# Weight products of 256 columns read from other places in SBUF, and eight transpose groups moved behind the last gate's rows

## The chip, the cores and the metric

One core of a Trainium2 chip runs the whole program in one launch. The metric is device time in microseconds (us). The kernel before takes 2344.75 us as the median of three runs (2341.22, 2344.75 and 2345.06).

## The reference

A two-layer trunk on x of 256 tokens by 2048 features, all in float32. Each layer is a mixer and an MLP, each of them ahead of it normed, scaled and shifted by a conditioning vector:

```
for l in (0, 1):
    sh1, sc1, g1, sh2, sc2, g2 = split(silu(c) @ ada_w[l] + ada_b[l], 6)
    h = rms_norm(x, norm1_g[l]) * (1 + sc1) + sh1
    x = x + g1 * mixer_l(h)          # layer 0: mLSTM and retention heads; layer 1: sparse attention
    h = rms_norm(x, norm2_g[l]) * (1 + sc2) + sh2
    x = x + g2 * (square(relu(h @ mlp_w1[l])) @ mlp_w2[l])     # 2048 -> 8192 -> 2048
```

Most of the work is products of h with weight matrices of 2048 rows, the widest of them mlp_w1 and mlp_w2.

## The kernel before, in words

**Two-part products.** Activations lie transposed: a tile `hs` holds for 128 features the 256 tokens twice, columns 0 to 255 the high part (float32 rounded to fp32r) and columns 256 to 511 the low part (the rest). A weight tile comes by DMA into `raw` (128 rows, up to 1024 columns), ScalarE rounds it into `wh` (L232) and VectorE writes the rest into `wl` (L234), both in `wsplit`. A product then takes high by high, high by low and low by high. There are two forms of it, and all their matmuls have line L124:

- `tmul`: 128 weight columns from `wh` are loaded into TensorE and multiply the 512 columns of `hs`; then 128 from `wl` multiply its first 256. Two matmuls, "a pair" below. The first MLP product and most of the second of layer 0 run so.
- `nmul2`: three matmuls of 256 columns, `wh` by the high part, `wh` by the low part, `wl` by the high part. "A triple" below. The mixers' projections into and out of the heads (`segment`, `out_groups`, the index and query products of layer 1), the first products of a layer's part (`entry`) and two of eight tiles of `residual` in layer 0's MLP run so.

In `nmul` (the value columns in `linear_n` and at L1116 on, and all of `result`) the weights are the moving operand instead, 512 columns at a time.

**Places.** The `hs` tiles, the `wh` tiles and the `wl` tiles all start at addresses that leave the same rest by 256 bytes. `wh` has 64 columns (256 bytes) of room beyond its 1024, and `place[0]` (L226) says how many columns behind its start the high part is written: 0 in both mixers, in layer 0's value products and in `result`, and 48 (192 bytes) in the MLPs from `entry` to the end of mlp_w1, and in layer 0 through mlp_w2. `wl` has no such room.

**Order.** Each engine runs its instructions in the order in which the program lists them. `linear` walks over pairs of 128-row blocks of the weights; after each output tile of a block it calls `side()`, which takes one entry from the list `pending` (None: do nothing). Small work is put there in pieces. `Fill` fetches the conditioning weights `ada_w` in between, one block of 512 KB per due slot, and VectorE sums them with the condition (`acc`, L402).

**The last gate.** In layer 1's MLP the last 2048 numbers of the conditioning (`ada_rows`, two halves `hf`) must stand in rows over all tokens. Each half takes two matmuls of `ones` by `acc`, in plain float32 with 512 columns (L124, shown as M<-acc,c), put into `pending` three entries apart.

**Turning the residual.** The last product leaves its output by tokens, so x, which lies by features, is turned: `turn(c)` for c from 0 to 3, each two groups of four 128 by 128 transposes (L579, M<-c,xT) with copies by ScalarE and VectorE. They are queued before mlp_w1's second column group, each behind twelve empty entries.

Of the kernel before, what the change touches and what calls it, by code (L numbers as in the profile page):

```python
# [18 lines left out]
P = 128  # L19
# [75 lines left out]
def tile_trunk(ctx: ExitStack, tc: tile.TileContext, io, out):  # L95
# [127 lines left out]
    def held_back():  # L223
        return tc.issue_after(behind[0]) if behind else nullcontext()

    place = [0]  # L226

    def wsplit(raw, n):
        wh = wp.tile([P, 1024 + 64], F32R, tag="wh", name="wh")[:, place[0]:place[0] + 1024]
        wl = wp.tile([P, 1024], F32R, tag="wl", name="wl")  # L230
        with tc.high_priority(offset=60):
            S.copy(wh[:, :n], raw[:, :n])  # L232
            with held_back():
                last_split[0] = V.tensor_tensor(wl[:, :n], raw[:, :n], wh[:, :n].bitcast(F32), op=OP.subtract)  # L234
        return wh, wl
# [9 lines left out]
            o += b - a  # L245
        return raw

    def wload(W, k0, kper, cols):

        raw = wp.tile([P, 1024], F32, tag="raw", bufs=4, name="raw")  # L250
        wfetch(raw, W, k0, kper, cols)
        return wsplit(raw, kper * sum(b - a for a, b in cols))

    def tmul(o, h, wh, wl, c, m, start, stop):

# [43 lines left out]
    def linear_n(W, nk, kper, c0_, hget, evac, fill=None, k1=0):  # L299

        bs = [lbank() for _ in range(2)]
        for k0 in range(k1, nk, kper):
            wh, wl = wload(W, k0, kper, [(c0_, c0_ + 512)])
            if fill is not None:
                fill()
            for t in range(2):
                for kk in range(kper):
                    k = k0 + kk
                    nmul(bs[t], hget(k), t, wh[:, kk * 512:(kk + 1) * 512], wl[:, kk * 512:(kk + 1) * 512],
                         k == k1, k == nk - 1)  # L310
                side()
        for t in range(2):
            evac(t, bs[t])
# [46 lines left out]
    def ada_rows(acc, hf):  # L360

        r = wp.tile([P, 1024], F32, tag="ada", bufs=3, name="grow")
        SP.dma_start(r[0:1, :], io["ada_b"][1:2, 5 * D + hf * 1024:5 * D + (hf + 1) * 1024])
        V.tensor_tensor(acc[0:1, :], acc[0:1, :], r[0:1, :], op=OP.add)

        def part(q):
            b = bank(3)
            mm(b, ones, acc[:, q * 512:(q + 1) * 512])
            S.copy(acc[:, q * 512:(q + 1) * 512], b)

        def end():
            part(1)
            grow[hf] = acc
            open_.pop(0)

        open_.append(acc)
        pending.extend([None] * 2 + [lambda: part(0), None, None, None, end])

    landing = []

# [115 lines left out]
    def entry(W, cols, tiles, norm, l, n, held, late, out, done):  # L496


        w = sum(b - a for a, b in cols)
        us = norm.plain(l, n)  # L500
        ws = []
        for k0 in range(0, 8, 2):
            tag, room = (("wh", 1088), ("wl", 1024))[k0 // 2 % 2]
            r = wp.tile([P, room], F32, tag=tag, bufs=4, name="wu")
            ws.append(wfetch(r, W, k0, 2, cols))
        norm.lengths(last_split[0].ins)
        hs, sums_ = [None] * KT, []
        for k0 in range(0, KT, 2):
            if k0 >= 8:
                wh, wl = wload(W, k0, 2, cols)  # L510
            for q, (c, m) in enumerate(tiles):
                for kk in range(2):
                    k = k0 + kk
                    if k < 8:
                        mm(held[q][0:m, 0:T + 1], ws[k0 // 2][:, kk * w + c:kk * w + c + m], us[k][:, 0:T + 1],
                           k == 0, k == 7)
                    else:
                        nmul2(q % 2)(late[q // 2], hs[k], wh, wl, kk * w + c, m, k == 8 and q % 2 == 0, k == KT - 1)
            side()
            if k0 == 6:  # L520
                for k in range(8, KT):
                    hs[k] = norm.normed(l, n, k)
                for q, (c, m) in enumerate(tiles):
                    b, s = held[q], small.tile([P, 1], F32, tag="shs", name="shs")
                    V.tensor_tensor(out[q], b[0:m, 0:T], norm.rb[0:m], op=OP.mult)
                    S.copy(s[0:m], b[0:m, T:T + 1])
                    sums_.append(s)
        behind.clear()
        for q, (c, m) in enumerate(tiles):
            V.scalar_tensor_tensor(out[q], late[q // 2][0:m, q % 2 * T:q % 2 * T + T], sums_[q][0:m], out[q],  # L530
                                   op0=OP.add, op1=OP.add)
            done(q)
        for k in range(8):
            hs[k] = norm.normed(l, n, k)
        return hs
# [56 lines left out]
    def result(W, hget):  # L592
# [2 lines left out]
        held = [lbank() for _ in range(4)] + [bank(i) for i in range(4)]  # L595
        last = []
        for k in range(n):
            w = [wload(W, k, 1, [(c, c + 1024)]) for c in (0, 1024)]
            h = hget(k)
            if k >= n - 2:  # L600
                last.append((k, h, w))
                continue
            for t in range(2):
                for c in range(4):
                    wh, wl = (v[:, c % 2 * 512:c % 2 * 512 + 512] for v in w[c // 2])
                    nmul(held[4 * t + c], h, t, wh, wl, k == 0, False)
# [11 lines left out]
    def mlp(l, before, fill, norm):  # L618
        with ExitStack() as es:
# [13 lines left out]
            def squared(i, a):  # L633
# [1 line left out]
                S.activation(z[i], a, AF.Square)  # L635

            free[:] = [3]
            place[0] = 48
            hs = entry(io["mlp_w1"][l], [(0, 512)], [(j * P, P) for j in range(4)], before, l, 1,
                       [bank(0), bank(1), bank(2), lbank()], [lbank(), lbank()], [ztile(i) for i in range(4)],  # L640
                       lambda q: squared(q, z[q]))
            if l == 1:
                for c in range(4):
                    pending.extend([None] * 12 + turn(c))
            for g in range(1, DFF // 512):
                def evac(j, b, g=g):
                    a = tmp.tile([P, T], F32, tag="half", name="half")
# [5 lines left out]
            if l == 1:  # L653
                fill.flush()
                while pending:
                    side()
                place[0] = 0
                zp.tile([P, 24], F32, name="pad")
                result(io["mlp_w2"][l],
                       lambda k: split_to_hs(z[k], zp.tile([P, 2 * T], F32R, tag="zh", bufs=3, name="zh")))  # L660
                return
            residual(io["mlp_w2"][l], DFF // P, lambda k: split_to_hs(z[k]), shift(l, 5), norm, mlp_groups(),
                     2, fill)
            place[0] = 0
            fill.flush()
            free[:] = [0, 1, 2, 3]

# [23 lines left out]
    with ExitStack() as es:  # L691
# [3 lines left out]
        def wraw(name="raw"):  # L695
            tag = turns.pop(0)
            turns.append(tag)
            return wp.tile([P, 1088 if tag == "wh" else 1024], F32, tag=tag, bufs=4, name=name)[:, 0:1024]

        xn = [[wraw("xn") for _ in range(2)] for _ in range(2)]  # L700
        for t in range(2):
# [155 lines left out]
        def gates():  # L857
# [3 lines left out]
            V.tensor_scalar(gb, gb, 1.0 / 15.0, None, op0=OP.mult)  # L861
            wg = tmp.tile([P, KT, 8], F32, tag="diag", bufs=2, name="wg")
            SP.dma_start(wg, wE[:, 4096:4104].rearrange("(k p) c -> p k c", p=P))
            wgh, wgl = wsplit(wg.rearrange("p k c -> p (k c)"), KT * 8)
            gbk = bank()
            for k in range(KT):
                tmul(gbk, hs[k], wgh, wgl, k * 8, 8, k == 0, k == KT - 1)
# [48 lines left out]
                emat.append(E)  # L916


        qk = sums(7)
        for k in range(KT):  # L920
            if k >= 12:
# [192 lines left out]
    nb = [nb[2 * i:2 * i + 2] for i in range(3)]  # L1114
    q0b = bank(2)
    for k in range(PART, KT):  # L1116
        w = [wload(wE, k, 1, wcols[:1]), wload(wE, k, 1, wcols[1:])]
        fill()
        for s in range(3):
            for t in range(2):  # L1120
# [60 lines left out]
    with ExitStack() as es:  # L1181
# [5 lines left out]
        SP.dma_start(rb_, io["rel_bias"])  # L1187
        b = bank()
        mm(b[0:16, 0:384], rb_, c3[0:32, 256:640])
        bv = ap.tile([16, 384], F32, name="bv")  # L1190
        V.tensor_copy(bv, b[0:16, 0:384])
        bd = dram.tile([16, 384], F32, name="bd")
        SP.dma_start(bd, bv)
# [201 lines left out]
```

## Time and profile before

| | |
|---|---|
| median of three runs | 2344.75 us |
| the profiled execution | 2340.88 us |
| its span on the core | 2339.1 us |
| TensorE matmul busy | 2280.5 us (97%) |
| TensorE weight loads busy | 2033.0 us (87%) |
| VectorE busy | 1704.9 us (73%) |
| ScalarE busy | 1191.6 us (51%) |
| DMA, mean | 262 GB/s |
| mean granted TensorE clock | 0.992 of full speed |

Matmuls overlap in the records: one starts before the one ahead of it has ended, and its recorded time reaches over the next. What a matmul costs in a stream is therefore the time from its start to the next start, which a count of matmuls in a stretch, or the starts in a timeline, give. A count of a stretch also holds about two matmuls that started ahead of it.

The stretches of the run: mixer of layer 0 up to 595 us (its output product from about 502), MLP of layer 0 to 1316 (mlp_w1 to 953), mixer of layer 1 to 1617 (output product from 1542), MLP of layer 1 to the end (entry to 1644, mlp_w1 to 1986, then `result`).

### The profile page before, as it was taken

The numbers are of one execution on the slowest core, as the hardware profiler recorded it, in microseconds if no ns is written. First come the engines' busy times: TensorE is split into PE (matmuls) and PEld (weight loads), VectorE is DVE, ScalarE is ACT, GpSimd is POOL, SyncE is SP. The second block draws the span as 40 slices with busy tenths as digits, with TensorE's granted clock in tenths as the row PEclk, the third lists the DMA queues.
The fourth block names the chain that finished last, engine by engine and source line by source line (L and its number), as shares of the span: only waits on it lengthen the run. The fifth ranks groups of instructions, "written<-read, shape, count | busy, mean of one in ns | idle before, by whom it ended". The sixth has DMA issues, their size and how long they took to land.

```text
span 2339.1 us, 37507 instructions
## 1 busy us (share of the span) xinstructions
PE 2280.5 (97%) x14121; PEld 2033.0 (87%) x14121; DVE 1704.9 (73%) x2499; ACT 1191.6 (51%) x2248; POOL 0.5 (0%) x8
## 2 busy tenths in 40 slices
PE   5899998999999999999999999999999999999999
PEld 3689888999988888999989899999988888888887
DVE  5768897995877777888988779865777455555555
ACT  3225455455555556655555445664655555444443
POOL 0000000000000000000000000000000000000000
PEclk8999999999999999999999999999999999999999
DMA  9998998996699999999899787645798665555554
GB/s 329 355 300 285 297 319 286 326 325 207 215 311 318 317 316 315 310 305 315 284 327 320 233 271 229 227 139 176 242 313 269 182 188 188 189 198 192 193 191 162
DMA packets 268909, 611.97 MB, mean 262 GB/s; under 512 B 26692, under 2 KB 95286, under 8 KB 268728
## 3 DMA queue, kind: packets, MB, share of 16 engines
q1 hardware_dynamic: 268728, 609.59, 78.2%
q8 instruction: 110, 1.80, 0.3%
q14 instruction: 71, 0.58, 0.1%
HBM read 607.38 MB, written 2.12 MB: 261 GB/s over the span
## 4 chain that ended last, share of the span: by engine, by line
PE 80%; DVE 9%; DMA 6%; issue 2%; ACT 2%; SPq 0%; DVEq 0%; ACTq 0%
PE L L124 49%; PE M L124 30%; DMA ada<-in_ada_w_dram 3%; DVE wl L234 3%; DMA raw<-in_even_w_in_dram 2%; DVE acc L402 1%; DVE acc L754 1%; PE M L332 1%; ACT wh L232 1%; DMA raw<-in_mlp_w_dram 1%; ACT junk L335 0%; DVE cv L1064 0%; DVE hs L207 0%; SPq L243 0%; PE M L737 0%
## 5 line engine op out<-in xcount | busy, mean ns | idle before, releaser
L234 DVE TENSOR_TENSOR wl<-raw,wh 128x1024 fp32r<-128x1024 f32 (+1 forms) x724 | 876.7, 1213 | 489.4 <-ACT wh L232 480.1
L232 ACT CAST wh<-raw 128x1024 fp32r<-128x1024 f32 (+1 forms) x724 | 753.7, 1042 | 830.6 <-PE M L124 442.1
L124 PE MATMUL L<-hs,wh 128*128 128x256 f32 (+1 forms) x4608 | 1131.7, 324 | 6.5 <-ACT wh L232 4.2
L124 PE MATMUL L<-hs,wl 128*128 128x256 f32 x3120 | 874.8, 281 | 2.4 <-DVE wl L234 2.4
L124 PEld LDWEIGHTS L<-hs,wh 128*128 128x128 f32 x4608 | 772.1, 190 | 70.9 <-ACT wh L232 5.9
L124 PEld LDWEIGHTS L<-hs,wl 128*128 128x128 f32 x3120 | 591.0, 190 | 4.1 <-DVE wl L234 3.2
L124 PE MATMUL M<-hs,wh 128*128 128x512 f32 (+2 forms) x1816 | 518.6, 347 | 0.0
L402 DVE SCALAR_TENSOR_TENSOR acc<-ada,cond,acc 128x1024 f32<-128x1024 f32 x300 | 383.3, 1278 | 30.5 <-DMA ada<-in_ada_w_dram 30.0
L124 PE MATMUL M<-hs,wl 128*128 128x256 f32 (+2 forms) x1444 | 403.1, 279 | 0.0
L124 PEld LDWEIGHTS M<-hs,wh 128*128 128x128 f32 (+1 forms) x1816 | 313.7, 187 | 52.1 <-issue 1.6
L124 PEld LDWEIGHTS M<-hs,wl 128*128 128x128 f32 (+2 forms) x1444 | 269.2, 186 | 1.9 <-issue 1.0
L124 PE MATMUL L<-wh,zh 128*128 128x512 f32 x512 | 168.7, 389 | 0.0
L124 PE MATMUL M<-wh,zh 128*128 128x512 f32 x512 | 168.6, 389 | 0.0
L124 PEld LDWEIGHTS L<-wh,zh 128*128 128x128 f32 x512 | 96.0, 188 | 20.2 <-issue 0.3
L124 PEld LDWEIGHTS M<-wh,zh 128*128 128x128 f32 x512 | 96.2, 188 | 20.0
L335 ACT ACTIVATE junk<-M 128x128 f32<-128x128 f32 x210 | 55.2, 278 | 88.0 <-PE M L332 87.9
L124 PE MATMUL L<-wl,zh 128*128 128x512 f32 x256 | 99.7, 389 | 0.0
L124 PE MATMUL M<-wl,zh 128*128 128x512 f32 x256 | 99.6, 389 | 0.0
L754 DVE SCALAR_TENSOR_TENSOR acc<-ar,cond,acc 128x512 f32<-128x512 f32 x120 | 90.2, 751 | 4.8 <-DMA ar<-in_ada_w_dram 1.0
L634 ACT ACTIVATE half<-half 128x256 f32<-128x256 f32 x120 | 47.8, 411 | 28.6 <-DVE half L325 28.6
L124 PE MATMUL L<-hf,raw 128*128 128x256 f32 x224 | 53.3, 392 | 4.9 <-DMA raw<-in_even_w_in_dram 4.9
L124 PEld LDWEIGHTS L<-wl,zh 128*128 128x128 f32 x256 | 48.1, 188 | 10.2 <-DVE wl L234 0.3
(273 smaller groups left out, 1575.4 us busy)
## 6 DMA issues: line engine op xcount, KB each, us to landing
raw<-in_mlp_w_dram SPq DMA_DIRECT2D x504, 512.0 KB, 4.6
ada<-in_ada_w_dram SPq DMA_DIRECT2D x320, 512.0 KB, 5.3
raw<-in_even_w_in_dram SPq DMA_DIRECT2D x136, 256.0 KB, 5.4
ar<-in_ada_w_dram SPq DMA_DIRECT2D x64, 512.0 KB, 7.8
raw<-in_odd_w_in_dram SPq DMA_DIRECT2D x48, 512.0 KB, 4.5
raw<-in_even_w_out_dram SPq DMA_DIRECT2D x32, 512.0 KB, 5.3
raw<-in_odd_w_out_dram SPq DMA_DIRECT2D x32, 512.0 KB, 4.2
raw<-in_even_w_in_dram SPq DMA_DIRECT2D x28, 512.0 KB, 6.1
```

The source lines that it names most:

```text
L124: PE.matmul(o, a, b, start=start, stop=stop, skip_group_check=True)
L232: S.copy(wh[:, :n], raw[:, :n])
L234: last_split[0] = V.tensor_tensor(wl[:, :n], raw[:, :n], wh[:, :n].bitcast(F32), op=OP.subtract)
L332: PE.transpose(b[:, i * P:(i + 1) * P], t, ident)
L335: S.activation(j, b[:, i * P:(i + 1) * P], func, accum_out=dst[:, i:i + 1])
L402: V.scalar_tensor_tensor(acc, r, cond[:, kr:kr + 1], acc, op0=OP.mult, op1=OP.add)
L634: S.activation(a, a, AF.Relu)
L754: V.scalar_tensor_tensor(acc, ar[:, kr], cc, acc, op0=OP.mult, op1=OP.add)
```

## The change

Two things. First, `wl` gets the same 64 columns of room as `wh`, and the place becomes a pair of numbers (columns behind the start for `wh` and for `wl`). EVEN (0, 0) stays for the products of 512 columns with the weights moving and for the gates' eight columns. WIDE (48, 0) is what the MLP's pairs had. PAIRED (16, 48), 64 and 192 bytes, is new: it holds for the triples of both mixers from the query and key products of layer 0 on, and for every `entry`. Second, the turns of the residual leave their place ahead of mlp_w1 and follow in `pending` the rows of the last gate: chunks 0 and 1 the first half's, chunks 2 and 3 the second's. A small tile of layer 1, `bv`, moves into a buffer that later holds logits, which makes room.

```
-    place = [0]
-    def wsplit(raw, n):
-        wh = wp.tile([P, 1024 + 64], F32R, tag="wh", name="wh")[:, place[0]:place[0] + 1024]
-        wl = wp.tile([P, 1024], F32R, tag="wl", name="wl")
+    ROOM = 1024 + 64
+    EVEN, PAIRED, WIDE = (0, 0), (16, 48), (48, 0)
+    place = [EVEN]
+    def wsplit(raw, n, at=None):
+        a, b = place[0] if at is None else at
+        wh = wp.tile([P, ROOM], F32R, tag="wh", name="wh")[:, a:a + 1024]
+        wl = wp.tile([P, ROOM], F32R, tag="wl", name="wl")[:, b:b + 1024]
...
     def linear_n(W, nk, kper, c0_, hget, evac, fill=None, k1=0):
-            wh, wl = wload(W, k0, kper, [(c0_, c0_ + 512)])
+            wh, wl = wload(W, k0, kper, [(c0_, c0_ + 512)], EVEN)
...
     def ada_rows(acc, hf):
-        pending.extend([None] * 2 + [lambda: part(0), None, None, None, end])
+        pending.extend([None] * 2 + [lambda: part(0), None, None, None, end, None, None])
+        for c in (2 * hf, 2 * hf + 1):
+            pending.extend(turn(c))
...
     def entry(W, cols, tiles, norm, l, n, held, late, out, done):
-                wh, wl = wload(W, k0, 2, cols)
+                wh, wl = wload(W, k0, 2, cols, PAIRED)
...
     def mlp(l, before, fill, norm):
-            place[0] = 48
+            place[0] = WIDE
...
-            if l == 1:
-                for c in range(4):
-                    pending.extend([None] * 12 + turn(c))
...
             residual(io["mlp_w2"][l], DFF // P, lambda k: split_to_hs(z[k]), shift(l, 5), norm, mlp_groups(),
-            place[0] = 0
+            place[0] = PAIRED
...
+        place[0] = PAIRED
         qk = sums(7)
...
-        bv = ap.tile([16, 384], F32, name="bv")
+        bv = ap.tile([P, 384], F32, tag="lg", bufs=3, name="bv")[0:16]
```

The places move no instruction. The turns do. On TensorE, near the start of mlp_w1 in layer 1 before, the first of eight transpose groups stands among the pairs (c_78 is the identity, hs, wh and wl as above):

```order
L124 MATMUL L<-hs,wh 128x512
L124 MATMUL L<-hs,wl 128x256
L579 MATMUL M_18170<-c_78,xT 128x128 x4
L124 MATMUL L<-hs,wh 128x512
L124 MATMUL L<-hs,wl 128x256
```

All eight groups stood so, far ahead of the gate's rows; these pairs now follow each other without a transpose. On TensorE now, from the second of the first half's two matmuls for the gate's rows (the one with acc) on:

```order
L124 MATMUL M_18995<-acc,c_78 128x512
L124 MATMUL M_18998<-hs,wh 128x512
L124 MATMUL M_18998<-hs,wl 128x256
...
L124 MATMUL M_18985<-hs,wh 128x512
L124 MATMUL M_18985<-hs,wl 128x256
L583 MATMUL M_19020<-c_78,xT 128x128 x4
L124 MATMUL M_18990<-hs,wh 128x512
L124 MATMUL M_18990<-hs,wl 128x256
```

Six pairs lie between that matmul and the first transposes, and eight pairs between the first and the second matmul of the rows. Four transpose groups follow each half's rows.

## Rows read from the trace of the kernel before

**Rows 1.** The page's chain that ended last: shares by engine, then by line.

```profile
PE 80%; DVE 9%; DMA 6%; issue 2%; ACT 2%; SPq 0%; DVEq 0%; ACTq 0%
PE L L124 49%; PE M L124 30%; DMA ada<-in_ada_w_dram 3%; DVE wl L234 3%; DMA raw<-in_even_w_in_dram 2%; DVE acc L402 1%; DVE acc L754 1%; PE M L332 1%; ACT wh L232 1%; DMA raw<-in_mlp_w_dram 1%; ACT junk L335 0%; DVE cv L1064 0%; DVE hs L207 0%; SPq L243 0%; PE M L737 0%
```

**Rows 2.** Busy time by stretch; first line names the columns, x counts instructions.

```profile
core 0: us, PE busy (x) PEld busy (x) DVE busy (x) ACT busy (x) POOL busy (x), PEclk, DMA share, GB/s
120.00:330.00 210.00, 203.30 (x1251) 180.06 (x1250) 167.55 (x239) 101.19 (x177) 0.10 (x1) 0.99 0.91 296
330.00:502.00 172.00, 163.34 (x1294) 160.10 (x1293) 153.92 (x281) 80.05 (x170) 0.00 (x0) 0.98 0.95 320
502.00:595.00 93.00, 93.00 (x769) 92.54 (x768) 58.10 (x86) 45.95 (x88) 0.00 (x0) 1.00 0.72 236
1316.00:1542.00 226.00, 222.83 (x1744) 211.51 (x1743) 192.25 (x509) 130.96 (x321) 0.00 (x0) 1.00 0.68 222
1542.00:1617.00 75.00, 75.00 (x626) 74.87 (x625) 38.71 (x54) 36.43 (x71) 0.00 (x0) 1.00 0.64 196
1644.00:1735.00 91.00, 91.00 (x545) 80.49 (x544) 69.73 (x79) 53.74 (x91) 0.00 (x0) 1.00 0.82 279
1735.00:1986.00 251.00, 251.00 (x1426) 218.74 (x1425) 143.14 (x150) 137.21 (x227) 0.00 (x0) 1.00 0.68 214
```

**Rows 3.** Chain of waits by line: 120 to 330, 330 to 502, 502 to 595, 1316 to 1542.

```profile
by line: DMA ada<-in_ada_w_dram 20.7%; PE L L124 12.4%; DVE wl L234 12.1%; PE M L124 11.7%; issue 10.9%; DMA raw<-in_even_w_in_dram 9.0%; DVE acc L402 7.6%; DVE cv L1064 4.7%; SPq L243 2.5%; DVE v L686 2.4%; ACT wh L232 1.2%; DVE mt L900 0.
by line: PE L L124 23.1%; DMA raw<-in_even_w_in_dram 15.6%; DMA ada<-in_ada_w_dram 11.4%; DVE wl L234 9.7%; issue 8.8%; DVE acc L402 6.2%; ACT wh L232 3.1%; PE M L124 2.5%; ACT junk L335 2.2%; PE M L1012 1.8%; DVE hs L207 1.4%; PE M L332 1.
by line: PE L L124 95.2%; PE M L124 2.8%; PE M L1012 1.1%; PE M L332 1.0%
by line: PE L L124 57.6%; PE M L124 9.8%; DVE wl L234 5.6%; issue 2.8%; DVE sc L1272 2.5%; ACT wh L232 1.8%; DVE m L1271 1.7%; ACT lg L1302 1.6%; PE M L332 1.5%; DVE lg L1290 1.3%; ACT lg L1299 1.2%; DVE acc L402 1.1%; DVE lg L1295 1.0%; DV
```

**Rows 4.** TensorE alone in four unbroken streams: triples, pairs, entry's triples, pairs.

```profile
core 0: us, PE busy (x), PEclk, DMA share, GB/s
550.00:590.00 40.00, 40.00 (x335) 1.00 0.61 189
700.00:750.00 50.00, 50.00 (x296) 1.00 0.92 315
1633.00:1643.00 10.00, 10.00 (x87) 1.00 0.62 170
1762.00:1812.00 50.00, 50.00 (x288) 1.00 0.82 270
```

**Rows 5.** Timeline of TensorE in layer 1's entry: start us, us, engine, line, operation.

```profile
1331.29 0.40 PE L124 MATMUL M<-hs,wh 128*128 128x256 f32 x2
...
1331.65 0.39 PE L124 MATMUL M<-hs,wh 128*16 128x256 f32 x2
...
1331.99 0.39 PE L124 MATMUL M<-hs,wh 128*16 128x256 f32 x2
```

**Rows 6.** Timeline of TensorE around the gate's first rows in mlp_w1 of layer 1.

```profile
1733.35 0.39 PE L124 MATMUL L<-hs,wh 128*128 128x512 f32 x1
...
1733.69 0.39 PE L124 MATMUL L<-hs,wh 128*128 128x512 f32 x1
...
1734.04 1.02 PE L124 MATMUL M<-acc,c 128*128 128x512 f32 x2
...
1735.24 0.40 PE L124 MATMUL L<-hs,wh 128*128 128x512 f32 x1
...
1735.60 0.40 PE L124 MATMUL L<-hs,wh 128*128 128x512 f32 x1
```

**Rows 7.** Timeline of TensorE around one transpose group, seventy microseconds earlier.

```profile
1664.64 0.60 PE L579 MATMUL M<-c,xT 128*128 128x128 f32 x4
...
1665.43 0.39 PE L124 MATMUL L<-hs,wh 128*128 128x512 f32 x1
...
1665.77 0.39 PE L124 MATMUL L<-hs,wh 128*128 128x512 f32 x1
```

More of the change, by code (lines that the diff above doesn't have):

```diff
@@ L246, in wfetch, with wload @@
         return raw
-    def wload(W, k0, kper, cols):
+    def wload(W, k0, kper, cols, at=None):
         raw = wp.tile([P, 1024], F32, tag="raw", bufs=4, name="raw")
         wfetch(raw, W, k0, kper, cols)
-        return wsplit(raw, kper * sum(b - a for a, b in cols))
+        return wsplit(raw, kper * sum(b - a for a, b in cols), at)
     def tmul(o, h, wh, wl, c, m, start, stop):
@@ L502, in entry @@
         for k0 in range(0, 8, 2):
-            tag, room = (("wh", 1088), ("wl", 1024))[k0 // 2 % 2]
-            r = wp.tile([P, room], F32, tag=tag, bufs=4, name="wu")
+            r = wp.tile([P, ROOM], F32, tag=("wh", "wl")[k0 // 2 % 2], bufs=4, name="wu")
             ws.append(wfetch(r, W, k0, 2, cols))
@@ L597, in result @@
         for k in range(n):
-            w = [wload(W, k, 1, [(c, c + 1024)]) for c in (0, 1024)]
+            w = [wload(W, k, 1, [(c, c + 1024)], EVEN) for c in (0, 1024)]
             h = hget(k)
@@ L663, in mlp @@
                      2, fill)
-            place[0] = 0
+            place[0] = PAIRED
             fill.flush()
@@ L697, in wraw @@
             turns.append(tag)
-            return wp.tile([P, 1088 if tag == "wh" else 1024], F32, tag=tag, bufs=4, name=name)[:, 0:1024]
+            return wp.tile([P, 1024 if tag == "raw" else ROOM], F32, tag=tag, bufs=4, name=name)[:, 0:1024]
         xn = [[wraw("xn") for _ in range(2)] for _ in range(2)]
@@ L863, in gates @@
             SP.dma_start(wg, wE[:, 4096:4104].rearrange("(k p) c -> p k c", p=P))
-            wgh, wgl = wsplit(wg.rearrange("p k c -> p (k c)"), KT * 8)
+            wgh, wgl = wsplit(wg.rearrange("p k c -> p (k c)"), KT * 8, EVEN)
             gbk = bank()
@@ L1116, in tile_trunk @@
     for k in range(PART, KT):
-        w = [wload(wE, k, 1, wcols[:1]), wload(wE, k, 1, wcols[1:])]
+        w = [wload(wE, k, 1, c, EVEN) for c in (wcols[:1], wcols[1:])]
         fill()
```

## The prediction, made before the changed kernel was run

> **What bounds the kernel now.** I read the chain that ended last first [rows 1]: 79% of the span is TensorE at L124, the line of all weight products, so what a product costs from its start to the next start is most of the time. The busy times by stretch come next [rows 2]: from 502 to 595 us, from 1542 to 1617 and in all of mlp_w1 of layer 1 (1644 to 1986) TensorE is busy without a gap, at a granted clock of 1.00, the 2.4 GHz level; from 120 to 502 the DMA share is 0.91 to 0.95 and TensorE has gaps. The chain of each stretch says how far a shorter product would move the end there [rows 3]: L124 is 98% of it from 502 to 595, 67% from 1316 to 1542, but 26% from 330 to 502 and 24% from 120 to 330, where DMAs, VectorE's low parts and issue make up most of the rest.
>
> Then the pace inside unbroken streams [rows 4]. About two of each count began ahead of the window. Mixer triples with both parts in the input's place: 333 in 40 us, 120 ns each, 360 per triple. Pairs in layer 0's mlp_w1: 294 in 50 us, 340 ns per pair. Both forms read 768 moving columns, so the same columns cost 20 ns more as a triple. The triples of the entry, whose high parts lie 192 bytes on and whose low parts lie in the input's place: 85 in 10 us, 117.6 each, 353 per triple. And the last row of the group: pairs of layer 1's mlp_w1, same code and same clock as the 340 ones, 286 in 50 us, 350 per pair.
>
> Two timelines say where these differences come from. In layer 1's entry, still with every part in the input's place for the small tiles, a triple with 128 weight columns starts 0.36 us ahead of the next, one with 16 weight columns 0.34 [rows 5]: the moving columns are the same, and it is the loading of weights beside them that costs the 20 ns. In mlp_w1 of layer 1 the pairs go at 0.34 until the first plain-float32 matmuls for the gate's rows, and at 0.36 (350 ns, by the count) from the first pairs behind them [rows 6]; the last of [rows 4] shows them still so, and 1735 to 1986 holds some 710 pairs in 251 us [rows 2], 353 each with the second half's rows among them. Behind a transpose group the pairs go at 0.34 [rows 7]. So there are two steady paces, and what ran last before the stream picks one.
>
> **The places.** They remove and add no instruction. Triples that get the new places: 140 in layer 0's query and key products (10 blocks of 14), 64 and 384 in its segments, 256 in its output product, 32 in layer 1's entry, 384 in its index and query products, 256 in its output product, and 64 in the two MLP entries: 1580. Pairs keep their place; the low-part buffers move by whole multiples of 256 bytes, and `wh`'s buffers, which are spaced that way already, show no pace of their own within the counted streams, so I cost this at nothing. Products with moving weights and the gates keep theirs.
>
> No row has parts at 64 and 192 bytes, so the price of a triple there is bounded. Fast side: 340, from the 16-column triple [rows 5] and the pairs [rows 4]. Slow side: 370, which is today's 360 plus the 10 ns that the slow pace adds to the pairs [rows 4]. Today's 360 and the entry's 353 lie between. The value that I take is 346.5, midway between 353 and 340: the entry's row is the nearest one, there one of the two parts is off the input's place and a third of the 20 ns is gone, and now both are. That is 13.5 ns per triple of the mixers and 6.5 per triple of the MLP entries.
>
> What of it moves the end, by the chain's shares [rows 3]: the two output products, all, 512 x 13.5 = 6.9 us. Layer 1's 416 others, 0.67 x 416 x 13.5 = 3.8. The 448 of the segments, 0.26 x 448 x 13.5 = 1.6; there a TensorE that is early waits for weights, with the DMAs at 320 GB/s and a share of 0.95 [rows 2]. The 140 ahead of them, 0.24 x 140 x 13.5 = 0.5. The entries, 64 x 6.5 = 0.4. Sum 13.2 us.
>
> Here a rule speaks against the change. The rows say that loading 128 columns instead of 16 costs the product beside it 20 ns per triple [rows 5]. The Trainium skill (TensorE: Matmul & The Clock Gate, Step-by-step: what each phase is for) says that TensorE has two independent read ports to SBUF, and that loading the next weights takes no read bandwidth from the running matmul. By it no place could matter, and this term would be 0 instead of 13.2; the trace does not agree, and I go by the trace, but the rule's outcome is the first rival below.
>
> **The turns.** Eight groups of four transposes, with eight copies of ScalarE more than VectorE's eight, leave the start of mlp_w1 and come back in the same stretch: the same number at the same price, beside pairs in both places. Their eight copies on ScalarE and four on VectorE are hidden by a TensorE that never waits there, with VectorE busy 143 of 251 us and ScalarE 137 [rows 2]; the `ada` buffers that they borrow delay the gate's weights by some steps, and the DMA share of 0.68 to 0.82 leaves room for that. If that cover went, the price would be a wait of TensorE for weights of a few us at most, since all eight groups take under 4 us of TensorE (0.45 each, by the 0.79 from the group's start to the second pair behind it less a 0.34 pair [rows 7]).
>
> What the move does change is the last thing that runs before each long stream of pairs. Now the transposes come six pairs behind the second rows matmul of each half. If they set the pace to 340 as they do in [rows 7], the slow pace lasts from the first rows matmul to the first transposes, 14 pairs, twice. Between 1735 and 1986 there are some 710 pairs (1426 matmuls [rows 2], less the rows' and the window's edge). The two paces differ by 349.7 - 340.1 = 9.6 ns [rows 4]: (710 - 28) x 9.6 = 6.5 us, all on the path. Its bounds: nothing, if the transposes only keep a fast pace and cannot restore one, since all groups that the trace shows behind pairs of mlp_w1 came into a fast stream; and 6.8 if they restore it at once.
>
> **The sum.** 13.2 + 6.5 = 19.7 us less than the profiled execution's 2340.9 gives 2321. That execution lies 3.9 below the median of the three runs; from the middle of both, 2342.8, it is **2323 us**, which I predict. Its own range is 2311 to 2332: at the fast end triples at 340, all of the gain of 1316 to 1542 and half of that of 120 to 502 (10.2 + 8.3 + 5.9 + 0.8 + 6.5 = 31.7), at the slow end the entry's 353 everywhere and 6.5.
>
> **Rivals.** First: the places do nothing, triples stay at 360. For it: in the stream of triples nothing but the start address of the weights changes, and 128 columns of 4 bytes sweep over 512 bytes wherever they start. Against it: the entry's 353 with only that changed. Time: 2342.8 - 6.5 = 2336. It is what the rule of the Trainium skill cited above would give (TensorE: Matmul & The Clock Gate, the same section).
>
> Second: the transposes do not restore the pace, or the entry's new triples hand the slow one to the pairs. For it: no row shows a slow stream that became fast within mlp_w1, and the early transposes that followed the entry are gone, so that a slow start would last from 1644 to 1735, 545 matmuls [rows 2] or, without 32 transposes, some 255 pairs, 2.5 us, and I take as much again for layer 0. Against it: the pace behind all transposes is the same. Time: 2342.8 - 13.2 = 2330, up to 2335.
>
> Third, the other side: the new places meet worse than the old. The low parts, which sat in the input's place, are the middle product's neighbours; if loading them 192 bytes on, or the high parts 64 on, keeps falling on the columns that the product beside it reads, a triple goes to 370. A longer product is covered by nothing in the output products and less by DMAs elsewhere: 576 x 10 + 0.9 x 416 x 10 + 0.7 x 588 x 10 = 13.6 us more, less 6.5: 2350. It decides from about 365 ns per triple on, where the turns' 6.5 are used up. Against it: 360 is an unvarying 120 per matmul, and the one place tried was better.
>
> Fourth: neither part does anything, 2343.
>
> **Chances.** Forecast 0.55, first rival 0.13, second 0.14, third 0.12, fourth 0.06. Range for 8 in 10: 2310, the fast end, to 2340, which takes in the first two rivals and leaves out most of the last two. A measurement tells some 0.2%, 4.7 us, from no change, so faster means below 2340.1: all of the forecast, 0.11 of the first and 0.13 of the second, together 0.79; within 0.2% 0.11 (the fourth, and the rims of the others), slower 0.10.
>
> **What would show it.** A stream of mixer triples in the output products with 343 to 355 in 40 us instead of 333 tells the first step right; still 333 tells the first rival, 325 the third. In mlp_w1 of layer 1 the starts of pairs should be 0.36 apart for two short stretches behind the rows and 0.34 from the first transposes to 1986's counterpart; 0.36 throughout tells the second rival. The output products should shrink by 3 to 5 us each, 1316 to 1542 by about 4, and 330 to 502 by less than 3, with more of TensorE's waits ended by DMAs and VectorE. I am wrong if the pairs' pace in layer 0's MLP changes, or if 120 to 502 gives back more than half of its triples' gain.

## The result, and the profile after

| | before | after |
|---|---|---|
| median of three runs | 2344.75 us | 2326.86 us (2325.87 to 2327.96) |
| the profiled execution | 2340.88 us | 2326.86 us |
| TensorE matmul busy | 2280.5 us | 2255.0 us |

The ratio is 0.9927 with a 95% interval of 0.9912 to 0.9943: 17.9 us less by the medians, 14.0 by the two profiled executions. The predicted 2323 is 3.9 us off, well within its range, but the experiments below show two of its assumptions on the places off, in opposite directions, so that part of the nearness is luck.

TensorE alone, in the kernel after: busy time with the count of matmuls, granted clock, DMA share and GB/s. The stretches stand against those of [rows 4]; the fifth is later in the same mlp_w1.

```profile
core 0: us, PE busy (x), PEclk, DMA share, GB/s
548.00:588.00 40.00, 40.00 (x353) 1.00 0.62 193
700.00:750.00 50.00, 50.00 (x297) 1.00 0.93 323
1625.00:1635.00 10.00, 10.00 (x86) 1.00 0.55 159
1746.00:1796.00 50.00, 50.00 (x296) 1.00 0.88 302
1880.00:1930.00 50.00, 50.00 (x297) 1.00 0.65 195
```

The mixers' triples: 351 matmuls in 40 us instead of 333, 114 ns each; from start to start a triple takes 340 ns, apart from one delay of 0.2 us in that window (before 360, without a delay), as low as the pairs. The gain is 19.7 ns per triple, the mean over layer 1's output product. Layer 0's pairs are as they were. Layer 1's pairs, 350 before, go at 340 in both stretches. The 10 us of the entry tell little: one matmul is 1.2% of them.

What happens around the gate's rows is the next view, a timeline of TensorE after: start, duration, line, operation.

```profile
1722.27 0.39 PE L124 MATMUL L<-hs,wh 128*128 128x512 f32 x1
...
1722.61 0.39 PE L124 MATMUL L<-hs,wh 128*128 128x512 f32 x1
...
1722.96 1.02 PE L124 MATMUL M<-acc,c 128*128 128x512 f32 x2
...
1724.17 0.40 PE L124 MATMUL L<-hs,wh 128*128 128x512 f32 x1
...
1724.52 0.40 PE L124 MATMUL L<-hs,wh 128*128 128x512 f32 x1
...
1729.59 0.60 PE L583 MATMUL M<-c,xT 128*128 128x128 f32 x4
...
1730.38 0.40 PE L124 MATMUL M<-hs,wh 128*128 128x512 f32 x1
...
1730.73 0.40 PE L124 MATMUL M<-hs,wh 128*128 128x512 f32 x1
...
1731.08 0.39 PE L124 MATMUL M<-hs,wh 128*128 128x512 f32 x1
```

Starts of pairs are 0.34 apart ahead of the first matmul for the rows and 0.35 behind it (0.36 in [rows 6], where the count gives 350 ns all the same); right behind the first transposes they are still 0.35 apart for three pairs, and the count from 1746 on above shows 340. The slow pace now lasts little more than the 14 pairs of a half that the prediction counted.

Where the time came from, by the first instruction of each stage in the two traces (layer 0's output product from ScalarE's first split of `y`, layer 1's from its first split of `o`; some 55 and 48 triples of the work before still follow these splits and lie in the rows of the output products):

| stage | before us | after us | difference | predicted |
|---|---|---|---|---|
| start to the output product of layer 0 | 475.1 | 475.9 | +0.8 | -2.1 |
| output product of layer 0 | 120.3 | 117.6 | -2.7 | -3.5 |
| entry and MLP of layer 0 | 717.0 | 717.5 | +0.5 | -0.2 |
| layer 1 to its output product | 173.3 | 170.3 | -3.0 | -3.8 |
| output product of layer 1 | 131.6 | 129.0 | -2.6 | -3.5 |
| entry of layer 1's MLP | 26.5 | 26.1 | -0.4 | -0.2 |
| mlp_w1 of layer 1 | 340.6 | 333.9 | -6.7 | -6.5 |
| rest | 354.5 | 354.6 | +0.1 | 0 |

Every term of the mixers came out smaller than predicted, though each triple got 20 ns shorter where 13.5 were assumed. The chain of waits after, by line, for 330 to 502:

```profile
by line: DMA ada<-in_ada_w_dram 20.1%; DMA raw<-in_even_w_in_dram 13.5%; PE L L124 12.9%; DVE wl L237 11.3%; DVE acc L407 9.6%; issue 8.9%; PE M L124 2.8%; ACT wh L235 2.5%; DMA xn<-in_x_dram 2.2%; PE M L1154 2.1%; PE M L1013 1.9%; DVE hs L
```

From 330 to 502 L124 fell from 26% [rows 3] to 16%; the loads of conditioning weights (`ada`) rose from 11.4% to 20.1%. The segments' shorter triples were handed on as other waits there, for DMAs above all; how much of them the DMAs take is tried below.

The output products have a second loss. In each of them one wait of TensorE for VectorE stands out; before (start of the matmul behind the wait, and in brackets the wait):

```profile
500.52 0.47 PE L124 MATMUL L<-hs,wh 128*128 128x256 f32 x2 [1.25 <-DVE hf L180]
...
1511.06 0.92 PE L124 MATMUL M<-kT,qt 128*128 128x256 f32 x4 [1.54 <-DVE lg L1291]
```

and after:

```profile
501.40 0.76 PE L124 MATMUL L<-hs,wh 128*128 128x256 f32 x2 [2.25 <-DVE hf L180]
...
1506.55 0.92 PE L124 MATMUL M<-kT,qt 128*128 128x256 f32 x4 [2.26 <-DVE lg L1292]
...
1508.02 0.60 PE L124 MATMUL L<-hs,wh 128*128 128x256 f32 x2
```

The busy times by stretch around the two waits, after (us, busy and count of TensorE, its weight loads, VectorE, ScalarE and GpSimd, granted clock, DMA share, GB/s):

```profile
499.00:506.00 7.00, 4.75 (x29) 4.63 (x28) 6.44 (x17) 2.82 (x4) 0.00 (x0) 0.76 0.91 358
1506.00:1513.00 7.00, 6.45 (x39) 6.35 (x39) 6.24 (x31) 4.03 (x12) 0.00 (x0) 0.76 0.33 98
```

and before:

```profile
499.00:506.00 7.00, 5.75 (x46) 5.46 (x45) 7.00 (x17) 4.07 (x7) 0.00 (x0) 1.00 0.79 284
1506.00:1513.00 7.00, 5.46 (x39) 5.07 (x39) 6.60 (x38) 3.06 (x7) 0.00 (x0) 1.00 0.44 145
```

A granted clock of 0.76 over 7 us is 3.4 us at 0.5, the 1.2 GHz level, and the rest at 1.00. So TensorE had waited 2.25 and 2.26 us for VectorE where the clock fell, and 1.25 and 1.54 us at the same steps before, where it stayed at 1.00. The length of the wait does not decide it by itself. Two other waits of the kernel after:

```profile
346.11 0.33 PE L1013 MATMUL M<-c,yn 128*128 128x128 f32 x1 [1.66 <-ACT yn L1005]
...
409.49 0.33 PE L1013 MATMUL M<-c,yn 128*128 128x128 f32 x1 [2.27 <-ACT yn L1005]
```

and the clock around them (TensorE alone: us, busy and count, granted clock, DMA share, GB/s):

```profile
344.00:351.00 7.00, 5.34 (x31) 0.76 0.78 294
408.00:415.00 7.00, 5.51 (x44) 1.00 1.03 350
```

The shorter one goes with a fall, the longer one does not.

In layer 0 the wait ends 25.2 us behind the first split of `y` before and 25.3 after: the triples ahead of it gain nothing, they only make the wait longer. (The wait is not the places' alone: with the old places and the turns moved it was 2.03 us, at a clock of 1.00.) From its end to the first product of the MLP the stretch went from 95.1 to 92.3 us, 2.8 of the 256 x 19.7 ns = 5.0 of the output product. Of the 2.2 that are missing, 3.4 us at half the clock can cost up to 1.7.

### The profile page after: what moved, and what is told of

Read it like the earlier page. It is cut to its first block, busy times and chain, and to the rows that moved or that the text cites. A ratio compares the mean times of both kernels' runs of the same rounds, so it can differ in the third digit from the quotient of the medians.

```text
span 2325.1 us, 37502 instructions
## 1 busy us (share of the span) xinstructions
PE 2255.0 (97%) x14121; PEld 2008.9 (86%) x14121; DVE 1706.4 (73%) x2499; ACT 1190.4 (51%) x2248; POOL 0.5 (0%) x8
## 4 chain that ended last, share of the span: by engine, by line
PE 81%; DVE 8%; DMA 7%; issue 2%; ACT 2%; SPq 0%; DVEq 0%; ACTq 0%
PE L L124 48%; PE M L124 31%; DMA ada<-in_ada_w_dram 3%; DVE wl L237 2%; DMA raw<-in_even_w_in_dram 2%; DVE acc L407 2%; DVE acc L754 1%; DMA raw<-in_mlp_w_dram 1%; PE M L335 1%; ACT wh L235 1%; DMA xn<-in_x_dram 0%; DVE cv L1065 0%; ACT junk L338 0%; PE M L737 0%; SPq L246 0%
## 5 line engine op out<-in xcount | busy, mean ns | idle before, releaser
L237 DVE TENSOR_TENSOR wl<-raw,wh 128x1024 fp32r<-128x1024 f32 (+1 forms) x724 | 877.6, 1214 | 485.1 <-ACT wh L235 474.9
L124 PE MATMUL L<-hs,wh 128*128 128x256 f32 (+1 forms) x4608 | 1107.8, 321 | 6.7 <-ACT wh L235 4.4
L124 PE MATMUL L<-hs,wl 128*128 128x256 f32 x3120 | 866.3, 278 | 4.2 <-DVE wl L237 4.2
L124 PEld LDWEIGHTS L<-hs,wh 128*128 128x128 f32 x4608 | 762.2, 189 | 69.5 <-ACT wh L235 5.0
L124 PEld LDWEIGHTS L<-hs,wl 128*128 128x128 f32 x3120 | 587.9, 189 | 7.0 <-DVE wl L237 6.0
L124 PE MATMUL M<-hs,wh 128*128 128x512 f32 (+2 forms) x1816 | 514.8, 345 | 0.0
L124 PE MATMUL M<-hs,wl 128*128 128x256 f32 (+2 forms) x1444 | 401.4, 278 | 0.0
L124 PEld LDWEIGHTS M<-hs,wh 128*128 128x128 f32 (+1 forms) x1816 | 313.0, 186 | 50.8 <-issue 1.6
L124 PEld LDWEIGHTS M<-hs,wl 128*128 128x128 f32 (+2 forms) x1444 | 268.9, 186 | 1.9 <-issue 1.1
L124 PE MATMUL L<-wh,zh 128*128 128x512 f32 x512 | 168.6, 389 | 0.0
L124 PE MATMUL M<-wh,zh 128*128 128x512 f32 x512 | 168.5, 389 | 0.0
L124 PEld LDWEIGHTS L<-wh,zh 128*128 128x128 f32 x512 | 96.1, 188 | 20.3 <-issue 0.4
L124 PEld LDWEIGHTS M<-wh,zh 128*128 128x128 f32 x512 | 96.1, 188 | 20.0
L124 PE MATMUL L<-wl,zh 128*128 128x512 f32 x256 | 99.7, 390 | 0.0
L124 PE MATMUL M<-wl,zh 128*128 128x512 f32 x256 | 99.6, 389 | 0.0
L124 PE MATMUL L<-hf,raw 128*128 128x256 f32 x224 | 53.3, 392 | 4.4 <-DMA raw<-in_even_w_in_dram 4.4
L124 PEld LDWEIGHTS L<-wl,zh 128*128 128x128 f32 x256 | 48.1, 188 | 10.2 <-DVE wl L237 0.3
```

The costliest lines, as they stand in the source:

```text
L124: PE.matmul(o, a, b, start=start, stop=stop, skip_group_check=True)
```

## The experiments

Kernels without an interval were run once, or not against the kernel that they are set beside: their times are good to a few us, their counts in streams are much better.

**The two halves alone, and both again.** The theory: the parts act on different instructions, so each brings its own gain, and they add up. The rivals were a turn that works only with the new places, and places worth little.

The turns alone, on the kernel before:

```
     def ada_rows(acc, hf):
-        pending.extend([None] * 2 + [lambda: part(0), None, None, None, end])
+        pending.extend([None] * 2 + [lambda: part(0), None, None, None, end, None, None])
+        for c in (2 * hf, 2 * hf + 1):
+            pending.extend(turn(c))
...
-            if l == 1:
-                for c in range(4):
-                    pending.extend([None] * 12 + turn(c))
```

> The kernel before with the turns alone moved behind the gate's rows; every place stays 0 or 48. Theory (the transposes restore the fast pace of the pairs): mlp_w1 of layer 1 runs at 340 ns per pair behind the first transposes, 6.5 to 7 us less in all, about 2336; triples stay at 360. Rival (the gain of mlp_w1 came from the entry's new places, not from the transposes): pairs stay at 350 behind the rows and the time stays within 1 us of before. Rival (the transposes cost elsewhere what they give): pairs at 340 but under 3 us less in the time.

The places alone are the kernel after with exactly this edit reversed:

```
-        for c in (2 * hf, 2 * hf + 1):
-            pending.extend(turn(c))
...
+                for c in range(4):
+                    pending.extend([None] * 12 + turn(c))
```

> The changed kernel with the turns back at the start of mlp_w1; the new places stay. Theory: triples at 340 to 342, pairs behind the gate's rows at 350, time 6.5 to 7 us above the changed kernel, so about 10 to 12 us under before. Rival (the places are worth only the 7.3 us that the two profiles show outside mlp_w1 of layer 1): 7 us under before. Rival (places are worth the forecast's 13): 13 us under before.

Both parts, the kernel after again:

> The changed kernel itself on the same chip as the two halves, to see whether their gains add up. Theory (two separate things): its gain over before is that of e1_turns plus that of e2_places within 2 us, 17 to 18 us. Rival (they overlap): clearly less than the sum.

Measured against 2342.97 us (median of 13 runs of before): turns 2336.24, ratio 0.9972 [0.9961, 0.9984]; places 2332.81, 0.9954 [0.9940, 0.9967]; both 2327.82, 0.9932 [0.9920, 0.9945]. That is 6.7, 10.2 and 15.2 us; the halves' sum is 16.9, equal to both within their intervals and within the 2 us that were allowed, though 15.2 lies under the 17 to 18 expected. TensorE alone with the turns only:

```profile
550.00:590.00 40.00, 40.00 (x335) 1.00 0.64 195
1755.00:1805.00 50.00, 50.00 (x296) 1.00 0.89 307
```

and with the places only:

```profile
550.00:590.00 40.00, 40.00 (x353) 1.00 0.67 209
1755.00:1805.00 50.00, 50.00 (x288) 1.00 0.81 263
```

Each half changes the stream that it was said to change, and not the other: triples go from 333 to 351 in 40 us, pairs behind the rows from 286 to 294 in 50. One stream moved that neither half touches: with the turns only, the pairs of layer 0's mlp_w1 began at the slow pace and went over to the fast one:

```profile
645.00:690.00 45.00, 45.00 (x259) 1.00 0.91 312
700.00:750.00 50.00, 50.00 (x297) 1.00 0.91 312
```

257 matmuls in 45 us are 350 ns per pair, 295 in 50 are 339. Between the two stands a group of four transposes, here of the conditioning:

```profile
693.64 0.60 PE L332 MATMUL M<-c,acc 128*128 128x128 f32 x4
```

Up to there this kernel has the same program as the kernel before, whose pairs went at 340 from the start, and TensorE waited in neither from 600 to 694 us. So the same instructions can start at either pace, for a reason that no run shows, and transposes end the slow one here too.

**Is it the transposes, or what lies around them?** On the kernel before, one group of four transposes, whose result nobody reads, follows each half's rows; the turns stay early.

```
+        def again():
+            b = bank(3)
+            for i in range(4):
+                PE.transpose(b[:, i * P:(i + 1) * P], xT[:, 4 * hf + i, 0:P], ident)
+
-        pending.extend([None] * 2 + [lambda: part(0), None, None, None, end])
+        pending.extend([None] * 2 + [lambda: part(0), None, None, None, end, None, None, again])
```

> The kernel before, turns in their old place, with one more group of four transposes behind each half's rows whose result nobody reads. Theory (a transpose group by itself sets the pace of what follows): pairs at 340 from that group on, mlp_w1 of layer 1 some 5.5 us shorter (6.5 less two groups of 0.45). Rival (it takes the whole turn, its copies, or the missing early groups): pairs stay at 350 and mlp_w1 is 0.9 us longer.

2339.43 us. TensorE alone, ahead of the rows and behind the added group:

```profile
1705.00:1735.00 30.00, 30.00 (x174) 1.00 0.95 336
1755.00:1805.00 50.00, 50.00 (x296) 1.00 0.87 294
```

Behind the group 294 matmuls in 50 us: one unread group restores 340, so it takes neither the copies nor the rest of the turn. But mlp_w1 fell only from 340.6 to 337.5 us, 3.1 where 5.5 was expected, since the pairs ahead of the rows now ran at 349 (172 in 30 us). The timeline of TensorE shows where that began:

```profile
1700.74 0.39 PE L124 MATMUL L<-hs,wh 128*128 128x512 f32 x1
1702.58 0.39 PE L124 MATMUL L<-hs,wl 128*128 128x256 f32 x1 [1.45 <-DVE wl L234]
1702.80 0.39 PE L124 MATMUL L<-hs,wh 128*128 128x512 f32 x1
...
1703.15 0.40 PE L124 MATMUL L<-hs,wh 128*128 128x512 f32 x1
```

A wait of 1.45 us between the two matmuls of a pair, at a clock of 1.00, and the pairs behind it start 0.35 apart, up to the rows. In this run a mere pause, without a plain-float32 matmul, was followed by the slow pace too.

**Which of the two places pays?** Four kernels change one line of the kernel after, one number or two at a time; the first moves only the high parts:

```
-    EVEN, PAIRED, WIDE = (0, 0), (16, 48), (48, 0)
+    EVEN, PAIRED, WIDE = (0, 0), (16, 0), (48, 0)
```

> The changed kernel with only the high parts of the triples off the input's place (16 columns, 64 bytes; low parts at 0). A triple of the output products costs 360 ns with neither part off and 340 with both. Theory (each of the three products pays by the place of the weights that are loaded beside it, two of them high parts): 347. Rival (the high parts alone decide): 340. Rival (it takes both, one pays for all): 353 to 360.

only the low parts, PAIRED = (0, 48):

> The changed kernel with only the low parts of the triples off (48 columns, 192 bytes; high parts at 0). Theory (each product pays for itself, one of three loads is a low part): 353. Rival (the high parts alone decide): 360. Rival (the low parts decide): 340.

the high parts to the other place, PAIRED = (48, 0):

> The changed kernel with the triples at the place of the MLP's pairs (48, 0). The entries of the kernel before ran so, at 353 ns per triple. Theory (the place alone sets a stream's pace, whatever stage it is in): 353 in the output products too. Rival (the entry's 353 was the end of what its float32 products ahead had set): 360 or 340.

and the pairs in the triples' place, WIDE = (16, 48):

> The changed kernel with the pairs of mlp_w1 and of layer 0's mlp_w2 at the triples' new place (16, 48) instead of (48, 0). Triples stay at 340. Theory (340 per 768 columns is the floor of both forms, and the new place reaches it for a pair as well): pairs at 340, and the two triples in mlp_w2's steps fall from some 354 to 340, which is 256 x 9 ns or more, 2 to 4 us less than the changed kernel's 2326. It would also tell whether pairs at that place have the slow pace: 340 right behind the gate's rows would mean no. Rival (a pair wants another place than a triple): pairs at 345 or more, 1500 pairs x 5 ns or more than 7 us slower.

They took 2335.39, 2336.67, 2330.63 and 2356.93 us. Triples of layer 0's output product, and pairs of mlp_w1 of layer 0, as TensorE's counts have them; first (16, 0):

```profile
540.00:580.00 40.00, 40.00 (x330) 1.00 0.54 178
...
1565.00:1595.00 30.00, 30.00 (x257) 1.00 0.61 186
```

(0, 48):

```profile
540.00:580.00 40.00, 40.00 (x342) 1.00 0.56 184
```

(48, 0):

```profile
540.00:580.00 40.00, 40.00 (x342) 1.00 0.59 186
```

and the kernel with pairs at (16, 48), triples then pairs:

```profile
540.00:580.00 40.00, 40.00 (x353) 1.00 0.62 193
...
700.00:750.00 50.00, 50.00 (x285) 1.00 0.89 300
```

A triple takes 353 ns with only the low parts moved, as expected, 353 on average with the high parts at 48, as expected too, and 340 with both at (16, 48). With the high parts at 16 alone it takes 366 in layer 0 and 353 in layer 1 (255 matmuls in 30 us): worse than no move in one stream, better in the other, so triples too have two paces. The expected 347 was a miss, and the gains of the two parts do not add up from these. And 340 is no property of (16, 48) as such: there a pair costs 353 (283 matmuls in 50 us), 13 more than at (48, 0), and the kernel is 29 us slower than the kernel after: the rival was right. Of the places tried, the best one is another for each form of the product.

A fifth put the pairs in the input's place, WIDE = (0, 0):

> The changed kernel with the pairs of both MLPs in the input's place (0, 0). Pairs ran at 340 at (48, 0), with a second pace of 350 behind a disturbance, and at 353 at (16, 48). Theory (each form has its own good and bad places, and the input's place is a bad one for a pair as it is for a triple): 353 to 360 from entry on, with or without transposes ahead, 1500 pairs of mlp_w1 x 13 to 20 ns and more from mlp_w2, 25 to 45 us slower than the changed kernel. Rival (two loads per 768 columns are few enough that the place hardly matters, and 353 was special to (16, 48)): 340 to 350, at most 15 us slower.

2347.17 us, beside one run of before of 2345.48 and 19.4 over the kernel after's 2327.82 on another chip. Its pairs, in mlp_w1 of layer 0 and late in that of layer 1:

```profile
700.00:750.00 50.00, 50.00 (x285) 1.00 0.90 310
1900.00:1950.00 50.00, 50.00 (x291) 1.00 0.63 190
```

283 matmuls in 50 us are 353 ns per pair, 289 are 346: this place has two paces as well, and its fast one is still slower than the 340 of (48, 0). Neither theory's size was met; that the input's place is a bad one for pairs too was.

**Is it the DMAs that take the segments' gain?** Both kernels leave out 90 of the 96 loads of conditioning weights in layer 0's mixer, so the sums there are taken from stale blocks and the output is not the reference's; one keeps the triples in the input's place (PAIRED = (0, 0)), one is otherwise the kernel after.

```
-                    r = wp.tile([P, 1024], F32, tag="ada", bufs=3, name="ada")
...
-                    SP.dma_start(r, io["ada_w"][l, kr * P:(kr + 1) * P, cs:cs + 1024])
+                    if lag or kr == 0:
+                        r = wp.tile([P, 1024], F32, tag="ada", bufs=3, name="ada")
+                        SP.dma_start(r, io["ada_w"][l, kr * P:(kr + 1) * P, cs:cs + 1024])
```

> The changed kernel with all triples back at EVEN (0, 0), and with the fill of layer 0's mixer left out but for its first block of sixteen: 90 of 96 loads of 512 KB of conditioning weights are not done (VectorE sums the first block sixteen times instead), so that the mixer runs with about a third less DMA. The pair to d_paired. Theory (the mixer of layer 0 is held by DMA up to some 490 us): this alone shortens the stretch up to the MLP by 15 us or more. Rival (it is held by VectorE and TensorE's own waits): by under 5 us.

> As d_even (the same loads left out), with the triples at their new places. Theory (the 588 triples ahead of the output product gave nothing because the DMAs set the pace there): the stretch up to layer 0's MLP is now 8 to 14 us shorter than in d_even, where it was 2 to 3 us with the loads in, since 844 triples x 19.7 ns are 16.6. Rival (their chain is VectorE's and the heads', whatever the DMAs do): 2 to 5 us, as with the loads in.

2322.81 and 2307.69 us (four runs each). With the loads left out, the MLP of layer 0 begins at 583.95 us with the old place and at 576.29 with the new: 7.7 us apart. With the loads in, three runs with the old place have 594.81, 595.42 and 597.50, three with the new 592.54, 592.84 and 593.47, 3.0 between the means. The chain from 330 to 480, old place:

```profile
by line: PE L L124 63.4%; DVE wl L237 6.3%; PE M L124 6.1%; DMA raw<-in_even_w_in_dram 5.8%; issue 3.2%; PE M L335 2.7%; PE M L1014 2.5%; ACT wh L235 2.1%; DVE acc L408 1.8%; SPq L246 1.1%; ACT yn L1006 0.6%; PE M L1155 0.6%; DVE rs_a L179 
```

and new:

```profile
by line: PE L L124 46.9%; DVE wl L237 12.4%; issue 8.6%; DVE acc L408 7.7%; PE M L124 4.4%; PE M L335 2.7%; PE M L1014 2.5%; ACT wh L235 2.1%; DMA raw<-in_even_w_in_dram 2.1%; ACT yn L1006 1.6%; DVE cv L1077 1.2%; DVE hf L180 1.1%; DVE rs_a
```

So the DMAs do cover a part: the 844 triples up to there would give 844 x 19.7 ns = 16.6 us, 3.0 came with the loads in and 7.7 without them, just under the 8 to 14 expected. The loads account for 4.7 of the 13.6 us that did not arrive, a third. What covers the rest is open; with the new place VectorE's low parts and sums (L237, L408) rise from 8% to 20% of the chain, which points at them. And although L124 is 70% of the chain with the old place, under half of the triples' gain arrives. Removing the loads alone gained 12.0 us (from the mean of the three) where at least 15 were expected. Over the whole kernel the two differ by 15.1 us, since layer 1's triples have their places too.

The kernel with the old place also tells whether the room that `wl` got and the move of `bv` matter by themselves, as it has both. Its triples in layer 0's output product:

```profile
530.00:560.00 30.00, 30.00 (x252) 1.00 0.58 184
```

250 matmuls in 30 us, 360 ns per triple as before the change: for the pace of the triples they do not.

**A version with both places in one product.** In layer 0's mlp_w2 two of eight tiles are triples, in the pairs' place. This kernel splits a weight block into two pieces, 768 columns for pairs at (48, 0) and 256 for triples at (16, 48), two copies and two subtractions instead of one each.

```
+            S.copy(th[:, 304:1072], raw[:, 0:768])
+            S.copy(th[:, 16:272], raw[:, 768:1024])
...
+                V.tensor_tensor(tl[:, 320:1088], raw[:, 0:768], th[:, 304:1072].bitcast(F32), op=OP.subtract)
```

> The changed kernel with the tiles of layer 0's mlp_w2 cut in two: the columns of its pairs lie at (48, 0) and those of its two triples at (16, 48), by two instructions each of ScalarE and VectorE instead of one. Theory (each form at its own place runs at the floor of 340, also where they alternate): 256 triples fall from 353.4 to 340 and 768 pairs from 342.3 to 340, 5.2 us less than the changed kernel, about 2322. Rival (the pace carries over from one form to the next, or VectorE, 303 of 363 us busy there and now some 15 us more, holds it): within 1.5 us of the changed kernel or slower.

2320.97 us, ratio to before 0.9907 [0.9889, 0.9925]. By the medians it is 5.9 and 6.9 us under the two sets of runs of the kernel after, on other chips; not compared with it directly, and the two intervals of the ratio overlap, so that a gain over the kernel after is likely and not shown. In mlp_w2, TensorE's timeline after shows triples 0.35 apart:

```profile
1100.77 0.39 PE L124 MATMUL M<-hs,wh 128*128 128x256 f32 x2
...
1101.12 0.40 PE L124 MATMUL M<-hs,wh 128*128 128x256 f32 x2
```

and with the cut 0.34:

```profile
1101.55 0.39 PE L124 MATMUL M<-hs,wh 128*128 128x256 f32 x2
...
1101.89 0.39 PE L124 MATMUL M<-hs,wh 128*128 128x256 f32 x2
```

By the first instructions of the stages mlp_w2 takes 375.8 us where the kernel after took 378.0 and 379.9, so 2.2 to 4.1 less where 5.2 were expected, and layer 1's output product 127.0 where it took 129.0 and 128.7: in this profile the clock stayed at 1.00 from 1506 to 1513. So some 2 of these 6 us may be no work of the cut.

## Why the prediction was right

- **The places shorten the triples: right, its price too small.** 346.5 ns was taken, midway between two rows; 340 was measured, the end of the bounds named for it: 19.7 ns gained per triple instead of 13.5. The addresses that the weights are loaded from do change what a triple costs, from 340 to 366 ns. Why (16, 48) is good stays open, and the choice of it was in part luck: the prediction let each part that leaves the input's place take its share of the 20 ns, but the high parts at 16 alone gave 366 ns in one stream. The rule weighed against it (the Trainium skill, TensorE: Matmul & The Clock Gate, Step-by-step: what each phase is for: two independent read ports, so that weight loads take nothing from the running matmul) does not hold for these products, whose cost goes by the weights' place at a clock of 1.00. The first and third rivals fall.
- **What of it reaches the end: too much.** This is the step that failed, as far as one did: "what of it moves the end, by the chain's shares". Places alone gave 10.2 us, not 13.2, at the larger price. A share of the chain is what an engine holds of the path now; it is not what stays when that engine gets faster. In 120 to 502 us I let 26% and 24% through, and nothing came: the span to the output product is 475.9 us after, and 475.2 and 474.9 in two more traces with the new places, against 475.1, 474.4 and 477.1 in three with the old. The sign that the prediction named for this stretch ("if 120 to 502 gives back more than half of its triples' gain") asks for more than was forecast, not for less, so it could not catch this. In layer 1 ahead of the output product's row 3.0 us of some 368 x 19.7 = 7.2 arrived, 42% where the share was 67% (48 of the 416 triples stand behind that point).
- **"The two output products, all": wrong by half.** 2.7 and 2.6 us where 256 triples each gained 5.0, under the 3 to 5 named as the sign. VectorE's chains did not get shorter with the triples, TensorE waited longer, and then had half the clock for 3.4 us. What the half clock costs shows in layer 1 with places alone: the wait was 1.59 us, the clock stayed at 1.00, the stretch from the wait's end to the MLP took 102.6 us against 103.9 after (106.4 before), and 4.6 us arrived in the whole row.
- **The turns: right.** 6.5 us predicted, 6.7 measured both by the run with them alone and by mlp_w1 after. The step that no row could support, that transposes restore a fast pace within a slow stream, is shown by the unread group. The second rival falls. The copies and the gate's weights cost nothing visible. That what ran last before a stream picks its pace is shown for transposes and for the rows, not in general: layer 0's mlp_w1 began fast before and slow with the turns only, behind the same instructions.
- **The sum.** The forecast's places were 3.0 us too large and its turns 0.2 too small against the separate runs, of 19.7 in all. The fourth rival falls by the intervals. Two errors within the places, price 13.5 for 19.7 and passage, partly cancelled, which is why the total came so near. The slow end of the forecast's own range, 2332, does not follow from its terms: 353 ns everywhere with the same shares gives 6.6 us, and with the turns' 6.5 it is 2330.

## What to carry to other kernels

When a stream of identical instructions runs at two speeds in two places of one trace, at one clock, compare starts and not durations, look at operand addresses and at what ran last, and change one of them alone: 6% of a triple and 3% of a pair lay there, with no instruction more. Price such a gain stage by stage, and in a stage where the engine waits already, count nothing until the thing it waits for is gone, and then less than the chain's share. Watch whether a faster stretch lengthens the next wait, and at which clock the time behind it runs.

## What the runs showed of the hardware that was not expected

- The cost of the same 768 columns of fp32r product went from 340 to 366 ns with the start addresses of the two weight parts alone: triples 360 at (0, 0), 366 or 353 at (16, 0), 353 at (0, 48) and (48, 0), 340 at (16, 48); pairs 353 or 346 at (0, 0), 353 at (16, 48), 340 or 350 at (48, 0). The order of the places differs between the two forms; why is open.
- A stream keeps its pace for hundreds of products (pairs at 350 from the rows to the end of mlp_w1 before), is slow behind plain-float32 matmuls of 512 columns and, once, behind a pause of 1.45 us, and is back at 340 within a few pairs behind four transposes. That the pause alone did it was seen and not tested by itself. Once a stream of pairs was slow from its start, behind the same instructions that left it fast in another trace.
- A wait of some 2 us can go with 3.4 us at a granted clock of 0.5, and its length alone does not tell: in the kernel after waits of 1.66, 2.25 and 2.26 us did and one of 2.27 us did not.
